# Strassen's seven block products for two in three tiles of the gate and up projections

## The chip, the core and the metric
The kernel runs on one NeuronCore of a Trainium2 chip. The metric is the device time of one execution in microseconds (us). Engines: TensorE (PE; its weight loads are shown apart, as PEld), VectorE (DVE), ScalarE (ACT), GpSimd (POOL), and SyncE (SP), whose queue issues most DMA transfers.

## The reference
One decoder block for 512 tokens of width 1024 in float32: sparse attention and an RWKV-7 branch side by side, merged by gates, then a SwiGLU feed-forward part with 2816 hidden columns. The change is in that last part:

```
hn = _rms_norm(h, ffn_norm[l])
gate, up = _split(hn @ w_gate_up[l], (FFN_HIDDEN, FFN_HIDDEN))
h = h + (jax.nn.silu(gate) * up) @ w_down[l]
```

## The kernel before
Every large product is made of three matmuls: each operand is split into a high part (a copy rounded to the type fp32r, by ScalarE) and a low part (the rest, a subtraction), and high x high, high x low and low x high are summed in PSUM. Weights come as one stream of chunks of 128x1024 (512 KB). `chunk` issues the DMA from SP's queue into one of two raw buffers, has ScalarE make the high part `w_hi`, and has VectorE (every third chunk) or GpSimd make the low part `w_lo`; three buffers each.

The stage around the change begins when the normed hidden state `hn` is there, transposed: 8 blocks of 128 channels by 512 tokens, in high and low parts `hnh` and `hnl`. The 2816 hidden columns are 22 tiles of 128. For a tile, `dense_t` runs 24 matmuls (8 blocks of channels, three each) of 512 columns for gate and 24 for up: weights are held, `hn` is streamed. ScalarE then takes silu of the gate bank (`gsig`), VectorE multiplies it by the up bank (L1108), ScalarE makes the high part `uh`, GpSimd the low part `ul` (L1112). The first three products (tile 0's gate and up, tile 1's gate) are run in halves of 256 columns, as `hn` becomes ready. The down product then holds parts of `uh` and `ul` and streams the weights, in two passes of 512 output columns, with four banks each; at its end VectorE adds the residual and SP writes the output.

PSUM has eight banks: three with tag "d", three "c", two "i". In the gate and up stage only "d" is used.

The order on TensorE is the order of the code (the streams of the attention and the recurrence are done by then). The order on the other engines is set by a scheduler, ahead of time, in one queue per engine; an engine takes its queue in turn. SBUF buffers of one tag are reused in a ring, and the next use waits for the last reader.

Of the kernel before, what the change touches and what calls it, by code (L numbers as in the profile page):

```python
# [10 lines left out]
F32 = mybir.dt.float32  # L11
# [22 lines left out]
UA = ("score", "relu", "widx_t", "tab", "ytile", "sg", "ag", "wa2", "seg", "am", "u32", "ht")  # L34
# [93 lines left out]
def hybrid_block(ctx: ExitStack, tc: tile.TileContext, x, first, rows, consts, lora, rel_bias, stream, out):  # L128
# [10 lines left out]
    def bank(tag, dt=F32, name=None):  # L139
        n = {"d": 3, "i": 2, "c": 3}[tag]  # L140
        return pp.tile([128, 512], dt, name=name or "ps_" + tag, tag=tag, bufs=n)
# [90 lines left out]
    def chunk(k, n):  # L232
# [7 lines left out]
        eng = nc.vector if i >= POOL_ONLY and i % 3 == 0 else nc.gpsimd  # L240
# [7 lines left out]
    def w_tile(n):  # L248

        r = []  # L250
        for _ in range(n // 128):
            r += chunk(1024 // n, n)
        return r
# [734 lines left out]
    def products(wt, w2):  # L988
# [104 lines left out]
        fp = ctx.enter_context(tc.tile_pool(name="ffn", bufs=1))  # L1093
        up = []
        for j in range(NF):
            if j == 0:
                outs = [(bank("d"), w_tile(128)) for _ in range(3)]
                yield from dense_halves(outs, hn, "hn")
                (ps, _), (pu, _), (ps_1, _) = outs
            else:  # L1100
                ps = ps_1 if j == 1 else bank("d")
                if j > 1:
                    yield from dense_t(ps, w_tile(128), slice(0, 128), hn)
                pu = bank("d")
                yield from dense_t(pu, w_tile(128), slice(0, 128), hn)
            g = unit("gsig")
            nc.scalar.activation(g, ps, AF.Silu)
            nc.vector.tensor_mul(g, pu, g)  # L1108
            uh = fp.tile([128, S], F32R, name="uh", tag="uh", bufs=NF)
            ul = fp.tile([128, S], F32R, name="ul", tag="ul", bufs=NF)  # L1110
            nc.scalar.activation(uh, g, AF.Copy)  # L1111
            nc.gpsimd.tensor_sub(ul, g, uh)  # L1112
            up.append((uh, ul))

        for g in range(2):
            cs = slice(g * 512, g * 512 + 512)
            pss = [bank(tag) for tag in (("c", "c", "c", "i") if g == 0 else ("d", "d", "d", "i"))]
            for k0 in range(0, NF, 2):
                wt = chunk(2, 512)
                last = k0 == NF - 2  # L1120
                for t, k in [(t, k) for t in range(NT) for k in range(2)] if last else [(t, k) for k in range(2)
                                                                                   for t in range(NT)]:
                    j, ts = k0 + k, slice(t * 128, t * 128 + 128)
                    uh, ul = up[j][0][:, ts], up[j][1][:, ts]
# [3 lines left out]
                    if j == NF - 1:  # L1128
                        nc.vector.tensor_add(ht[t][g], pss[t], ht[t][g])
                        nc.sync.dma_start(out[t * 128:(t + 1) * 128, cs], ht[t][g])  # L1130

# [92 lines left out]
```

## Time and profile before

| | |
|---|---|
| Time, median of 3 runs | 917.99 us (917.96 to 919.47) |
| The profiled execution's own time | 918.64 us |
| Its span, first to last instruction | 916.9 us |
| Busy: PE, DVE, ACT, POOL | 901.0, 407.5, 345.3, 392.7 us |
| Gate and up products after the halves | 570.08 to 793.15 us |
| Down product to the end | 793.15 to 916.9 us |
| TensorE's granted clock, mean | 0.999 of full (2.4 GHz) |

A matmul's record is longer than the time from its start to the next one's, since matmuls overlap. So a product's time is read from starts, not from the sum of records. An engine's idle time costs something only where TensorE waits for it.

### The profile page before, as it was taken

How to read it: one execution, taken by the hardware profiler on the slowest of the kernel's cores; microseconds unless marked ns; L12 is line 12 of the kernel's file. 1: busy time of each engine (PE TensorE's matmuls, PEld its weight loads, DVE VectorE, ACT ScalarE, POOL GpSimd, SP SyncE). 2: the span in 40 equal slices, each digit the busy share in tenths (PEclk: the TensorE clock that was granted, in tenths of full speed). 3: DMA queues.
4: the chain of work that ended last, by engine and by line, in shares of the span. 5: the costliest groups of instructions: out<-in, count | busy, mean ns of one | idle time of the engine just before them, and what ended most of it. 6: DMA issues, size and time to landing. Idle time of an engine off the chain costs nothing.

```text
span 916.9 us, 13642 instructions
## 1 busy us (share of the span) xinstructions
PE 901.0 (98%) x5550; PEld 760.6 (83%) x5550; DVE 407.5 (44%) x782; ACT 345.3 (38%) x548; POOL 392.7 (43%) x265
## 2 busy tenths in 40 slices
PE   6999999999999999999999999999999999999998
PEld 5988898888787788888888999888888888888886
DVE  5389996785877456756417242111111111110101
ACT  5564575554734333333243243223322232211210
POOL 6477762322572444353338323444344443423321
PEclk9999999999999999999999999999999999999999
DMA  6321332111122111012323222323323222232421
GB/s 239 91 87 46 114 120 71 46 47 38 67 71 60 62 42 48 1 48 81 127 92 94 91 69 82 110 90 110 92 92 107 90 102 93 92 105 88 152 92 46
DMA packets 24173, 77.77 MB, mean 85 GB/s; under 512 B 2869, under 2 KB 4366, under 8 KB 24112
## 3 DMA queue, kind: packets, MB, share of 16 engines
q1 hardware_dynamic: 20688, 72.49, 24.8%
q10 hardware_dynamic: 3424, 4.43, 1.8%
q8 instruction: 43, 0.70, 0.3%
q14 instruction: 18, 0.15, 0.1%
HBM read 74.53 MB, written 2.38 MB: 84 GB/s over the span
## 4 chain that ended last, share of the span: by engine, by line
PE 80%; DVE 3%; POOL 2%; issue 1%; ACT 1%; POOLq 0%; ACTq 0%; DVEq 0%
PE ps_d L162 60%; PE ps_c L162 10%; PE ps_i L162 8%; PE ps_c L169 2%; DVE kr L716 1%; DVE sg L681 1%; POOL w_lo L243 1%; POOL bb L710 0%; PE ps_d L169 0%; POOL ag L719 0%; DVE lg L577 0%; POOL ss L328 0%; DVE xs L330 0%; ACT xs L326 0%; DVE sg L633 0%
## 5 line engine op out<-in xcount | busy, mean ns | idle before, releaser
L243 POOL TENSOR_TENSOR w_lo<-w_raw,w_hi 128x1024 fp32r<-128x1024 f32 (+1 forms) x94 | 223.4, 2377 | 309.9 <-ACT w_hi L239 302.8
L239 ACT ACTIVATE w_hi<-w_raw 128x1024 fp32r<-128x1024 f32 x129 | 136.7, 1060 | 349.3 <-PE ps_d L162 223.0
L162 PE MATMUL ps_d<-hnl,w_hi 128*128 128x512 f32 (+1 forms) x376 | 141.3, 376 | 0.4 <-DVE hnl L338 0.4
L162 PE MATMUL ps_d<-xnl,w_hi 128*128 128x512 f32 (+2 forms) x360 | 141.4, 393 | 0.0
L162 PE MATMUL ps_d<-hnh,w_hi 128*128 128x512 f32 (+1 forms) x376 | 141.2, 376 | 0.0
L162 PE MATMUL ps_d<-hnh,w_lo 128*128 128x512 f32 (+1 forms) x376 | 141.2, 376 | 0.0
L162 PE MATMUL ps_d<-xnh,w_lo 128*128 128x512 f32 (+2 forms) x360 | 140.5, 390 | 0.5 <-POOL w_lo L243 0.5
L162 PE MATMUL ps_d<-xnh,w_hi 128*128 128x512 f32 (+2 forms) x360 | 140.7, 391 | 0.0
L243 DVE TENSOR_TENSOR w_lo<-w_raw,w_hi 128x1024 fp32r<-128x1024 f32 x37 | 48.2, 1302 | 131.1 <-ACT w_hi L239 130.0
L1108 DVE TENSOR_TENSOR gsig<-ps_d,gsig 128x512 f32<-128x512 f32 x22 | 15.2, 692 | 155.0 <-PE ps_d L162 154.3
L162 PEld LDWEIGHTS ps_d<-hnl,w_hi 128*128 128x128 f32 x376 | 70.8, 188 | 13.2 <-DVE hnl L338 0.6
L162 PEld LDWEIGHTS ps_d<-hnh,w_hi 128*128 128x128 f32 x376 | 70.8, 188 | 12.9
L162 PEld LDWEIGHTS ps_d<-hnh,w_lo 128*128 128x128 f32 x376 | 70.7, 188 | 12.8
L162 PEld LDWEIGHTS ps_d<-xnh,w_lo 128*128 128x128 f32 x360 | 68.2, 189 | 12.3 <-issue 1.2
L162 PEld LDWEIGHTS ps_d<-xnl,w_hi 128*128 128x128 f32 x360 | 68.2, 189 | 11.8 <-issue 2.1
L162 PEld LDWEIGHTS ps_d<-xnh,w_hi 128*128 128x128 f32 x360 | 68.3, 190 | 10.7 <-issue 1.2
L1112 POOL TENSOR_TENSOR ul<-gsig,uh 128x512 fp32r<-128x512 f32 x22 | 31.6, 1437 | 24.0 <-ACT uh L1111 20.4
L811 POOL COPY rr<-eye 128x512 f16<-128x512 f16 x20 | 12.6, 635 | 58.2 <-PE ps_i L162 57.3
L162 PE MATMUL ps_d<-w_hi,mh 128*128 128x256 f32 x120 | 34.0, 284 | 0.0
L162 PE MATMUL ps_d<-w_hi,ml 128*128 128x256 f32 x120 | 34.0, 283 | 0.0
L162 PE MATMUL ps_d<-w_lo,mh 128*128 128x256 f32 x120 | 34.0, 283 | 0.0
L584 ACT ACTIVATE lg<-lg,mx,qrs 128x128 f32<-128x128 f32 (+3 forms) x32 | 20.9, 652 | 24.9 <-DVE mx L583 24.9
(294 smaller groups left out, 1712.5 us busy)
## 6 DMA issues: line engine op xcount, KB each, us to landing
w_raw<-in_stream_dram SPq DMA_DIRECT2D x129, 512.0 KB, 3.5
xa<-in_x_dram SPq DMA_DIRECT2D x4, 512.0 KB, 5.9
ht<-in_x_dram ACTq DMA_DIRECT2D x8, 256.0 KB, 3.7
out_dram<-ht SPq DMA_DIRECT2D x8, 256.0 KB, 2.4
toep<-bias_table ACTq DMA_DIRECT2D x8, 128.0 KB, 3.6
gain<-in_rows_dram ACTq DMA_DIRECT2D x2, 256.0 KB, 3.8
con<-in_consts_dram SPq DMA_DIRECT2D x1, 321.0 KB, 6.8
bias_table<-tab ACTq DMA_DIRECT2D x1, 276.0 KB
```

The costliest lines, as they stand in the source:

```text
L162: nc.tensor.matmul(o, w, r, **kw)
L169: nc.tensor.transpose(o, src, idn)
L239: nc.scalar.activation(hi, raw, AF.Copy)
L243: eng.tensor_sub(lo[:, o:o + n_], raw[:, o:o + n_], hi[:, o:o + n_])
L584: nc.scalar.activation(lg, lg, AF.Exp, scale=scale, bias=mx[:, 2:3], accum_out=den[:, h:h + 1])
L681: nc.vector.tensor_tensor_scan(cum, seg, cum, 0.0, op0=OP.mult, op1=OP.add)
L716: nc.vector.tensor_mul(KR[:, :, 0::3], v4(zrp), d3)
L811: nc.gpsimd.tensor_copy(two(R, 1), eye16.rearrange("q (g w s) -> q g w s", w=2, s=s)[:, None, :, 1] .to_broadcast([128, H, 64 // s, s]))
L1108: nc.vector.tensor_mul(g, pu, g)
L1112: nc.gpsimd.tensor_sub(ul, g, uh)
```

## The change
With the gate columns a11, a12 (first and second half of the channels) and the up columns a21, a22 of a tile, and the four blocks b of `hn` (half the channels by half the tokens), gate and up are a 2x2 block product. Strassen's form (Winograd's variant) makes it from seven block products instead of eight, with sums of blocks on both sides.

- `seven_sides`, once: VectorE rebuilds `hn` in float32 (`hnf`, L1227), makes four differences t1 to t4 of its blocks (`tf`, L1236), which ScalarE and VectorE split into high and low parts (`th`, `tl`, L1238 and L1239).
- Tiles 0, 1 and every tile j with j % 3 == 2 stay as they were ("plain"), but their low parts of weights are all on VectorE from tile 2 on. The other 13 tiles (3, 4, 6, 7, ... 18, 19 and 21) are Strassen tiles. For each, the gate chunk comes into `w_raw`, the up chunk into a ring of its own (`wu_raw`); VectorE makes s1 to s4 (L1149 to L1152); seven weight blocks of 128x512 are split, high part on ScalarE (L1155), low part on VectorE (L1156).
- Each of the seven products (`product`) is 12 matmuls with 256 columns. They use four banks: three banks get a second product after the first was read. The sums of products (L1176 to L1192) are on VectorE, two reads on ScalarE are silu and one a copy, and VectorE multiplies gate by up (L1195, L1196).
- All eight PSUM banks are used in turn (`next_bank`).
- The result `up` is kept in float32. The down product splits it again where it is used, in both passes: high part on ScalarE (L1206), low part on VectorE (L1207), in a ring of three buffers, which is that of `wu_raw`.

On TensorE, the place where one product follows another; `hnh` and `hnl` are parts of `hn`, the brackets name whose semaphores are waited for (Activation is ScalarE, Pool is GpSimd, DMAHW a DMA queue). Before, at the switch from a tile's gate to its up product:
```order
L162 MATMUL ps_d<-hnh,w_hi 128x512
L162 MATMUL ps_d<-hnl,w_hi 128x512
L162 MATMUL ps_d<-hnh,w_lo 128x512
L162 MATMUL ps_d<-hnh,w_hi 128x512 [waits Activation_49]
L162 MATMUL ps_d<-hnl,w_hi 128x512
L162 MATMUL ps_d<-hnh,w_lo 128x512 [waits Pool_49]
```
and now, at the end of a Strassen tile's first product and the start of its second, and where its sixth begins:
```order
L162 MATMUL ps_i<-hnl,w_hi 128x256
L162 MATMUL ps_i<-hnh,w_lo 128x256
L162 MATMUL ps_d<-th,w_hi 128x256 [waits Activation_49]
L162 MATMUL ps_d<-tl,w_hi 128x256
L162 MATMUL ps_d<-th,w_lo 128x256 [waits DVE_49]
...
L162 MATMUL ps_i<-hnh,s4h 128x256 [waits DVE_49]
L162 MATMUL ps_i<-hnl,s4h 128x256
L162 MATMUL ps_i<-hnh,s4l 128x256
```
A product has 12 matmuls of half the width in place of 24, so waits for other engines come more often: ten stand in such a tile.

On VectorE, two or three tiles of the gate and up stage before:
```order
L243 TENSOR_TENSOR w_lo<-w_raw,w_hi 128x1024 [waits DMAHW0_49,DVE_49,Activation_49]
L1108 TENSOR_TENSOR gsig<-ps_d,gsig 128x512 [waits PE_49,Activation_49]
L243 TENSOR_TENSOR w_lo<-w_raw,w_hi 128x1024 [waits DVE_49,DMAHW3_49,PE_49,Activation_49]
L1108 TENSOR_TENSOR gsig<-ps_d,gsig 128x512 [waits PE_49,Activation_49] x2
L243 TENSOR_TENSOR w_lo<-w_raw,w_hi 128x1024 [waits DMAHW6_49,DVE_49,Activation_49]
```
and now, from the first tile of a pair (its third and fourth product, `post`) into the second (`L1176` is its second product, `s` and `w_lo` are its weight blocks):
```order
L1182 TENSOR_TENSOR post<-ps_d,post 128x256 [waits DVE_49,PE_49]
L1149 TENSOR_TENSOR s<-wu_raw 128x512 [waits DMAHW6_49]
...
L1188 TENSOR_TENSOR upt<-ps_c,post 128x256 [waits PE_49]
L1156 TENSOR_TENSOR w_lo<-s,w_hi 128x512 [waits Activation_49]
L1152 TENSOR_TENSOR s<-w_raw,s 128x512 [waits DVE_49]
...
L1195 TENSOR_TENSOR u<-gsig,upt 128x256 [waits DVE_49]
L1156 TENSOR_TENSOR s4l<-s,s4h 128x512 [waits Activation_49]
L1176 TENSOR_TENSOR post<-ps_d,post 128x256 [waits PE_49,Activation_49]
L243 TENSOR_TENSOR w_lo<-w_raw,w_hi 128x1024 [waits DMAHW5_49,Activation_49]
L1179 TENSOR_TENSOR post<-ps_i,post 128x256 [waits DVE_49,PE_49]
L1182 TENSOR_TENSOR post<-ps_c,post 128x256 [waits DVE_49,PE_49]
L243 TENSOR_TENSOR w_lo<-w_raw,w_hi 128x1024 [waits DMAHW7_49,Activation_49]
```
The second tile's weight blocks are made between the reads of the first tile's products, and the first low part of the plain tile that follows stands ahead of L1179 and L1182, after whose reads TensorE may write the two banks again.

In the last pair (tiles 18 and 19), the same place on VectorE:
```order
L1176 TENSOR_TENSOR post<-ps_i,post 128x256 [waits PE_49,Activation_49]
L243 TENSOR_TENSOR w_lo<-w_raw,w_hi 128x1024 [waits DMAHW3_49,Activation_49]
L1207 TENSOR_TENSOR us<-u,us 128x512 [waits Activation_49]
L1179 TENSOR_TENSOR post<-ps_c,post 128x256 [waits DVE_49,PE_49]
L243 TENSOR_TENSOR w_lo<-w_raw,w_hi 128x1024 [waits DMAHW4_49,PE_49,Activation_49]
L1182 TENSOR_TENSOR post<-ps_d,post 128x256 [waits DVE_49]
```
Here a low part for the down product (L1207) and the second chunk of the plain tile have moved ahead of the two reads.

The core of the diff (line numbers L11xx and L12xx of the text above are those of the new kernel; L1107 to L1112 are those of the old one, where L1112 of the new one is the multiplication in `plain`):

```diff
-    def chunk(k, n):
+    def chunk(k, n, eng=None):
...
-        eng = nc.vector if i >= POOL_ONLY and i % 3 == 0 else nc.gpsimd
+        eng = eng or (nc.vector if i >= POOL_ONLY and i % 3 == 0 else nc.gpsimd)
...
+        four_k = lambda name, tag, n: fp.tile([128, 4, 256], F32R if tag == "tx" else F32, name=name, tag=tag, bufs=n)
+        tags = ["d", "c", "i", "d", "c", "d", "c", "i"]
         up = []
-        for j in range(NF):
-            if j == 0:
-                outs = [(bank("d"), w_tile(128)) for _ in range(3)]
-                yield from dense_halves(outs, hn, "hn")
-                (ps, _), (pu, _), (ps_1, _) = outs
-            else:
-                ps = ps_1 if j == 1 else bank("d")
-                if j > 1:
-                    yield from dense_t(ps, w_tile(128), slice(0, 128), hn)
-                pu = bank("d")
-                yield from dense_t(pu, w_tile(128), slice(0, 128), hn)
+        def up_rows(j):
+            if j % 2 == 0:
+                up.append(fp.tile([128, 2, S], F32, name="u", tag="u", bufs=NF // 2))
+            return up[j // 2][:, j % 2]
+        turn = [0]
+        def next_bank():
+            turn[0] += 1
+            return bank(tags[(turn[0] - 1) % 8])
+        def plain(j, ps, pu):
             g = unit("gsig")
             nc.scalar.activation(g, ps, AF.Silu)
-            nc.vector.tensor_mul(g, pu, g)
-            uh = fp.tile([128, S], F32R, name="uh", tag="uh", bufs=NF)
-            ul = fp.tile([128, S], F32R, name="ul", tag="ul", bufs=NF)
-            nc.scalar.activation(uh, g, AF.Copy)
-            nc.gpsimd.tensor_sub(ul, g, uh)
-            up.append((uh, ul))
+            nc.vector.tensor_mul(up_rows(j), pu, g)
+        outs = [(bank("d"), w_tile(128)) for _ in range(3)]
+        yield from dense_halves(outs, hn, "hn")
+        quads = seven_sides(fp, four_k, hn_)
+        plain(0, outs[0][0], outs[1][0])
+        pu = next_bank()
+        yield from dense_t(pu, w_tile(128), slice(0, 128), hn)
+        plain(1, outs[2][0], pu)
+        b11, b21, b22, t1, t2, t3, t4 = quads
+        def product(ps, hi, lo, b, first):
+            for k in range(4):
+                ks = slice(k * 128, k * 128 + 128)
+                xh, xl = b[k]
+                mm(ps, hi[:, ks], xh, start=first and k == 0, stop=False, skip_group_check=True)
+                mm(ps, hi[:, ks], xl, start=False, stop=False, skip_group_check=True)
+                mm(ps, lo[:, ks], xh, start=False, stop=k == 3, skip_group_check=True)
+        for j in range(2, NF):
+            if j % 3 == 2:
+                ps, pu = next_bank(), next_bank()
+                yield from dense_t(ps, w_tile(128, nc.vector), slice(0, 128), hn)
+                yield from dense_t(pu, w_tile(128, nc.vector), slice(0, 128), hn)
+                plain(j, ps, pu)
+                continue
+            wg = wp.tile([128, 1024], F32, name="w_raw", tag="w_raw", bufs=WBUFS[0])
+            wu = fp.tile([128, 1024], F32, name="wu_raw", tag="fx", bufs=3)
+            for w in (wg, wu):
+                nc.sync.dma_start(w, stream[at[0]])
+                at[0] += 1
+            a11, a12, a21, a22 = wg[:, 0:512], wg[:, 512:1024], wu[:, 0:512], wu[:, 512:1024]
+            s1, s2, s3, s4 = [unit("s") for _ in range(4)]
+            nc.vector.tensor_add(s1, a21, a22)
+            nc.vector.tensor_sub(s2, s1, a11)
+            nc.vector.tensor_sub(s3, a11, a21)
+            nc.vector.tensor_sub(s4, a12, s2)
+            def split(h, l, w):
+                nc.scalar.activation(h, w, AF.Copy)
+                nc.vector.tensor_sub(l, w, h)
+                return h, l
+            def two(wa, wb):
+                h = wp.tile([128, 1024], F32R, name="w_hi", tag="w_hi", bufs=WBUFS[1])
+                l = wp.tile([128, 1024], F32R, name="w_lo", tag="w_lo", bufs=WBUFS[2])
+                return split(h[:, 0:512], l[:, 0:512], wa), split(h[:, 512:1024], l[:, 512:1024], wb)
+            w11, ws2 = two(a11, s2)
+            ws1, ws3 = two(s1, s3)
+            w12, w22 = two(a12, a22)
+            ws4 = split(fp.tile([128, 512], F32R, name="s4h", tag="s4h", bufs=2),
+                        fp.tile([128, 512], F32R, name="s4l", tag="s4l", bufs=2), s4)
+            pa, pb, pc_, pd = [next_bank()[:, 0:256] for _ in range(4)]
+            post, upt, g = unit("post"), unit("upt"), unit("gsig")
+            u2, u3, c21, u2b = post[:, 0:256], post[:, 256:512], upt[:, 0:256], upt[:, 256:512]
+            product(pa, *w11, b11, True)
+            nc.scalar.activation(u2, pa, AF.Copy)
+            yield 0.0
+            product(pb, *ws2, t2, True)
+            nc.vector.tensor_add(u2, pb, u2)
+            yield 0.0
+            product(pd, *ws1, t1, True)
+            nc.vector.tensor_add(u3, pd, u2)
+            yield 0.0
+            product(pc_, *ws3, t3, True)
+            nc.vector.tensor_add(u3, pc_, u3)
+            yield 0.0
+            product(pa, *w12, b21, False)
+            nc.scalar.activation(g[:, 0:256], pa, AF.Silu)
+            yield 0.0
+            product(pd, *ws4, b22, False)
+            nc.vector.tensor_add(u2b, pd, u2)
+            nc.scalar.activation(g[:, 256:512], u2b, AF.Silu)
+            yield 0.0
+            product(pc_, *w22, t4, False)
+            nc.vector.tensor_add(c21, pc_, u2)
+            yield 0.0
+            u = up_rows(j)
+            nc.vector.tensor_mul(u[:, 0:256], g[:, 0:256], c21)
+            nc.vector.tensor_mul(u[:, 256:512], g[:, 256:512], u3)
         for g in range(2):
             cs = slice(g * 512, g * 512 + 512)
             pss = [bank(tag) for tag in (("c", "c", "c", "i") if g == 0 else ("d", "d", "d", "i"))]
             for k0 in range(0, NF, 2):
                 wt = chunk(2, 512)
+                uu = []
+                for k in range(2):
+                    s = fp.tile([128, 2, S], F32R, name="us", tag="fx", bufs=3)
+                    nc.scalar.activation(s[:, 0], up[k0 // 2][:, k], AF.Copy)
+                    nc.vector.tensor_sub(s[:, 1], up[k0 // 2][:, k], s[:, 0])
+                    uu.append(s)
                 last = k0 == NF - 2
                 for t, k in [(t, k) for t in range(NT) for k in range(2)] if last else [(t, k) for k in range(2)
                                                                                    for t in range(NT)]:
                     j, ts = k0 + k, slice(t * 128, t * 128 + 128)
-                    uh, ul = up[j][0][:, ts], up[j][1][:, ts]
+                    uh, ul = uu[k][:, 0, ts], uu[k][:, 1, ts]
                     mm(pss[t], uh, wt[k][0], start=(j == 0), stop=False)
                     mm(pss[t], uh, wt[k][1], start=False, stop=False)
                     mm(pss[t], ul, wt[k][0], start=False, stop=(j == NF - 1))
                     if j == NF - 1:
                         nc.vector.tensor_add(ht[t][g], pss[t], ht[t][g])
                         nc.sync.dma_start(out[t * 128:(t + 1) * 128, cs], ht[t][g])
+    def seven_sides(fp, four_k, a):
+        f = []
+        for q in range(4):
+            f.append(fp.tile([128, 2, S], F32, name="hnf", tag="u", bufs=NF // 2))
+            s = slice(2 * (q % 2), 2 * (q % 2) + 2)
+            nc.vector.tensor_add(f[q], a[0][q // 2][:, s], a[1][q // 2][:, s])
+        def block(k, t):
+            return [f[2 * k + e][:, :, 256 * t:256 * t + 256] for e in range(2)]
+        def minus(x, y):
+            d = four_k("tf", "u", NF // 2)
+            r = [d[:, 2 * e:2 * e + 2] for e in range(2)]
+            for e in range(2):
+                nc.vector.tensor_sub(r[e], x[e], y[e])
+            h, l = four_k("th", "tx", 8), four_k("tl", "tx", 8)
+            nc.scalar.activation(h, d, AF.Copy)
+            nc.vector.tensor_sub(l, d, h)
+            return r, [(h[:, k], l[:, k]) for k in range(4)]
+        d1, t1 = minus(block(0, 1), block(0, 0))
+        d2, t2 = minus(block(1, 1), d1)
+        _, t3 = minus(block(1, 1), block(0, 1))
+        _, t4 = minus(block(1, 0), d2)
+        as_is = lambda k, t: [(a[0][k][:, i, 256 * t:256 * t + 256], a[1][k][:, i, 256 * t:256 * t + 256])
+                              for i in range(4)]
+        return as_is(0, 0), as_is(1, 0), as_is(1, 1), t1, t2, t3, t4
```

## Rows read from the trace of the kernel before

**Rows 1.** The page: span, totals of the engines, and the chain that ended last.
```profile
span 916.9 us, 13642 instructions
PE 901.0 (98%) x5550; PEld 760.6 (83%) x5550; DVE 407.5 (44%) x782; ACT 345.3 (38%) x548; POOL 392.7 (43%) x265
...
PE ps_d L162 60%; PE ps_c L162 10%; PE ps_i L162 8%; PE ps_c L169 2%; DVE kr L716 1%; DVE sg L681 1%; POOL w_lo L243 1%; POOL bb L710 0%; PE ps_d L169 0%; POOL ag L719 0%; DVE lg L577 0%; POOL ss L328 0%; DVE xs L330 0%; ACT xs L326 0%; DVE sg L633 0%
```

**Rows 2.** Windows: us, then busy and (count) of PE, PEld, DVE, ACT, POOL; clock, DMA.
```profile
570.08:793.15 223.07, 223.07 (x987) 184.69 (x985) 30.99 (x34) 64.98 (x82) 95.23 (x49) 1.00 0.32 100
793.15:917.00 123.85, 119.84 (x529) 98.91 (x527) 13.58 (x15) 21.80 (x21) 34.77 (x15) 0.99 0.29 94
```

**Rows 3.** Timeline, 512-column matmuls (start, us, engine, line, names): first, last of a product, next stage.
```profile
570.08 0.40 PE L162 MATMUL ps_d<-hnh,w_hi 128*128 128x512 f32 x1
...
575.32 0.39 PE L162 MATMUL ps_d<-hnh,w_lo 128*128 128x512 f32 x1
575.82 0.69 DVE L1108 TENSOR_TENSOR gsig<-ps_d,gsig 128x512 f32<-128x512 f32 x1 [7.66 <-PE ps_d L162]
...
793.15 0.39 PE L162 MATMUL ps_c<-w_hi,uh 128*128 128x512 f32 x1
```

**Rows 4.** Timeline, 256-column matmuls, first and last of 44.
```profile
564.80 0.28 PE L162 MATMUL ps_d<-hnl,w_hi 128*128 128x256 f32 x1
...
569.96 0.28 PE L162 MATMUL ps_d<-hnh,w_lo 128*128 128x256 f32 x1
```

**Rows 5.** Window in the output projection, 256-column matmuls alone.
```profile
506.00:540.00 34.00, 34.00 (x285) 1.00 0.30 92
```

**Rows 6.** The matmul's line in 508 to 538 us (ns min/median/max, first and last start).
```profile
L162 PEld LDWEIGHTS ps_d<-w_lo,mh x84: 192/192/192, 507.9 to 537.8; 128*128 128x128 f32 x84
...
L162 PEldq EVENT_SEMAPHORE  x2: 51/51/51, 521.2 to 532.7; - x2
```

**Rows 7.** Timeline, a matmul that came late, and the next.
```profile
549.40 0.38 PE L162 MATMUL ps_d<-hnl,w_hi 128*128 128x256 f32 x1 [0.41 <-DVE hnl L338]
549.62 0.28 PE L162 MATMUL ps_d<-hnh,w_lo 128*128 128x256 f32 x1
```

**Rows 8.** VectorE's groups by form (busy us, mean ns); the first in gate and up alone.
```profile
L243 DVE TENSOR_TENSOR w_lo<-w_raw,w_hi 128x1024 fp32r<-128x1024 f32 x14 | 17.2, 1225 | 40.0 <-ACT w_hi L239 39.5
...
L1085 DVE TENSOR_TENSOR ht<-ps_d,ht 128x256 f32<-128x256 f32 x15 | 5.8, 419 | 18.9 <-PE ps_d L162 18.9
...
L717 DVE TENSOR_TENSOR kb<-ag,inv 128x512 f32<-128x512 f32 x4 | 2.8, 689 | 0.1
```

**Rows 9.** Timeline, VectorE instructions close behind each other.
```profile
134.44 0.68 DVE L446 MAX8 max<-score 128x8 f32<-128x512 f32 x1
135.04 0.19 DVE L583 TENSOR_SCALAR mx<-mx,qrs 128x1 f32<-128x1 f32 x1
...
137.99 0.34 DVE L573 SCALAR_TENSOR_TENSOR lg<-toep,qrs,ps_c 128x128 f32<-128x128 f32 x1
138.37 0.29 DVE L574 TENSOR_REDUCE mx<-lg 128x1 f32<-128x128 f32 x1
...
512.04 0.76 DVE L1085 TENSOR_TENSOR ht<-ps_d,ht 128x256 f32<-128x256 f32 x2 [2.12 <-PE ps_d L162]
```

**Rows 10.** ScalarE's group of 512-column copies.
```profile
L1111 ACT ACTIVATE uh<-gsig 128x512 fp32r<-128x512 f32 x22 | 13.9, 632 | 0.0
```

**Rows 11.** Timeline at the stage's start, VectorE's and ScalarE's.
```profile
556.51 1.43 DVE L338 TENSOR_TENSOR hnl<-ps_c,hnh 128x512 fp32r<-128x512 f32 x2 [0.71 <-ACT hnh L337]
...
564.45 1.06 ACT L239 ACTIVATE w_hi<-w_raw 128x1024 fp32r<-128x1024 f32 x1 [7.24 <-PE ps_d L162]
...
566.82 0.60 ACT L1107 ACTIVATE gsig<-ps_d 128x512 f32<-128x512 f32 x1
```

**Rows 12.** DMA issues by line (KB each, median us to landing), the page's and the stage's.
```profile
xa<-in_x_dram SPq DMA_DIRECT2D x4, 512.0 KB, 5.9
...
w_raw<-in_stream_dram SPq DMA_DIRECT2D x44, 512.0 KB, 3.5
```

More of the change, by code (lines that the diff above doesn't have):

```diff
@@ L33 @@
 UNITS, WBUFS = {"ua": 10, "uc": 8}, (2, 3, 3)
-UA = ("score", "relu", "widx_t", "tab", "ytile", "sg", "ag", "wa2", "seg", "am", "u32", "ht")
+UA = ("score", "relu", "widx_t", "tab", "ytile", "sg", "ag", "wa2", "seg", "am", "u32", "ht", "upt")
 SMALL = {"ss": 4, "max8": 3, "mx": 4}
@@ L246, in chunk, with w_tile @@
         return [(h3[:, j], l3[:, j]) for j in range(k)]
-    def w_tile(n):
+    def w_tile(n, eng=None):
         r = []
         for _ in range(n // 128):
-            r += chunk(1024 // n, n)
+            r += chunk(1024 // n, n, eng)
         return r
```

## The prediction

> **What bounds the kernel now.** I read the page's totals and chain first, then the stages by windows, then single matmuls and VectorE instructions in time. TensorE is busy 901.0 of a span of 916.9 us, and its matmul line L162 alone makes up 78% of the chain that ended last (60, 10 and 8% by the three kinds of PSUM bank) [rows 1]. The gate and up products run from 570.08 to 793.15 us, and in those 223.07 us TensorE is never idle, while VectorE works 30.99 us and ScalarE 64.98 us [rows 2]. So in that stage only the number and the spacing of the matmuls count. The stage holds 41 products of 24 matmuls, 984 in all: 223.07 / 984 = 0.2267 us from one start to the next, for matmuls of 512 columns. A matmul's record (0.39 us) is longer than its spacing, because matmuls overlap; all sums below go by spacing.
>
> Matmuls of 256 columns have a spacing of their own. From 564.80 to 569.96 us 43 of them follow each other with the same operands as here (weights held, activations streamed): 5.16 / 43 = 0.1200 us [rows 4]. In the output projection 285 fit into 34.00 us, 0.1193 us [rows 5]. Half the columns thus cost 53% of the time, not 50%.
>
> **The change, part by part.** *Matmuls.* Of the 22 column tiles, 13 (two of every three from tile 3 on) get seven products of 12 matmuls with 256 columns, 84, in place of 48 with 512. Per tile: 48 x 0.2267 = 10.88 us before, 84 x 0.1200 = 10.08 after, 0.80 saved; for 13 tiles 10.4 us. The stage becomes 360 x 0.2267 + 1092 x 0.1200 = 212.6 us. With 0.1193 instead it is 11.2 us saved; that is the lower end. An eighth of the columns goes away (84 x 256 against 48 x 512), 12.5% of 10.88 or 1.36 us; the dearer halves take 0.56 of that back.
>
> The new form has 36 more weight loads per tile. A load's record is 0.192 us, longer than the 0.12 us between two matmuls of 256 columns, and yet the spacing stays at 0.1193 to 0.1200 [rows 4 to 6]: the loads lie beside the matmuls. The Trainium skill, "TensorE: Matmul & The Clock Gate", section "The mechanism", says that a weight load overlaps with running matmuls only where its row group differs. All loads here fill the same rows, so by that rule they would lie on the path; the trace disagrees, with 0.12 us between matmuls whose loads alone take 0.19 us, and the rule is left a small chance below.
>
> *VectorE.* A Strassen tile gives it 11 instructions of 128x512 out of SBUF (4 sums of weight blocks, 7 low parts), 5 of 128x256 that read PSUM and 2 of 128x256 in SBUF. Rows of before show 0.689 us for the first kind and 0.419 for the second [rows 8]; with 0.419 for the third too the sum is 11 x 0.689 + 7 x 0.419 = 10.5 us per tile, above TensorE's 10.08. But instructions that follow each other without a dependence start sooner than the one before ends: 0.60 us apart for a 0.68 us one, and two of 128x256 take 0.76 together, so 0.34 apart; dependent ones stand 0.38 apart for a duration of 0.34, 0.04 behind the end [rows 9]. By spacing the tile costs 11 x 0.60 + 7 x 0.34 = 9.0 us. A plain tile costs it 2 x 1.14 + 0.60 = 2.9 (1.225 us [rows 8] less the same 0.08), so a group of three 20.9 us beside 31.0 us of TensorE. On average it fits; what matters is the order within a pair, since VectorE takes its instructions in turn. The Trainium skill, "VectorE: DVE Perf Modes", section "The DRAIN you can't avoid", has the next operation wait until the pipeline is empty. The spacing of 0.60 us under a duration of 0.68 does not agree with that; by that rule the tile costs the 10.5 us, which is the second case below.
>
> The tight place is the second tile of a pair. Time 0 is the start of the first one; products last 1.44 us; VectorE can read a product 0.50 us after the start of its last 512-column matmul, 0.11 after that record's end [rows 3], so with a 0.28 us record 0.27 us after the product's last spacing. VectorE in the order of the listing: L1182 waits for product 4 and starts at 6.03; s1 to s3 at 6.37, 7.10, 7.70; L1188 waits for product 6, 8.91; L1156 9.25; s4 9.85; the low part of s2 10.45, ends 11.14. The second tile's product 2 needs it at its third matmul, 10.08 + 1.44 + 0.24 = 11.76: 0.6 us to spare. On it goes: L1192 11.05, low part 11.39, L1196 11.99, low parts 12.33 and 12.93, L1195 13.53, low part of s4 13.87, L1176 14.47, the plain tile's 1024-wide low part 14.81, L1179 15.95 to 16.37. Product 6 writes again into the bank which L1179 reads and starts at 10.08 + 7.2 = 17.28: 0.9 us to spare. ScalarE copies in 0.63 us (512 columns) and 1.06 (1024) [rows 10, 11], seven copies of 512 and three reads of 256 columns per tile, well under the 10.08; its copy for the plain tile can start when product 2 is through at 13.2 and ends at 14.3, before VectorE wants it. So in five of the six pairs I cost the sums and splits at nothing; they lie beside the matmuls, and the cover is VectorE's overlap.
>
> The last pair (tiles 18 and 19) has two more instructions ahead of those reads, as the listing shows. The first low part for the down product (L1207, 0.60) leaves 0.3 of the 0.9 us. The second L243 stands ahead of L1182. Its raw chunk goes into the buffer that is free when the second tile's low part of a12 is made, at 13.0; a chunk lands 3.5 us later [rows 12], ScalarE 1.06, L243 1.23, L1182 0.42: 19.2 us, and product 7 waits for it at 10.08 + 8.64 = 18.72. Cost 0.5 us. A landing of 5.9 us, the slowest near row for such a chunk [rows 12], would make it 2.9; a quick one, nothing. I take 0.5, since 44 chunks have that median.
>
> *Preparation.* VectorE gets 4 sums of 1024, 8 differences of 512 and 4 low parts of 1024, after the last hnl, which ends at 556.51 + 1.43 = 557.94 [rows 11]. Eleven of them stand ahead of tile 1's low part: 4 x 1.14 + 7 x 0.62 = 8.9, then 1.23, ends 568.1; its first use is the third matmul from 570.08, 570.55. With full durations it ends 568.9. Hidden, with 1.6 us to spare or more. ScalarE makes the same first copy at 564.45, and the silu that frees the bank for 570.08 ran from 566.82 to 567.42 [rows 11]; one copy of 1.06 is put ahead of it, so it ends by 568.5. The other low parts are done near 578, and the first Strassen tile starts at 570.08 + 72 x 0.2267 = 586.4.
>
> *Down product.* Each of 44 row tiles is now split again there: ScalarE 0.63 and VectorE 0.69 per 12 matmuls (2.72 us), beside 1.06 and a third of 1.23 per two tiles. Both stay under half busy; the ring of three gives a buffer back two row tiles, 5.4 us, ahead of its need, and the refill takes about 1.5. Cost 0. GpSimd loses its low parts in the gate and up stage, which were on no path. SP moves the same 44 chunks in that stage; the up chunk of a Strassen tile gets a buffer of its own and is issued ahead, and the 100 GB/s of the stage [rows 2] stay.
>
> **Sum.** -10.4 + 0.5 = -9.9 us. Against the profiled execution's own 918.64 us (its span 916.9 and 1.7 around it) that is 908.7. The runs shown have a median 0.65 lower, 917.99, so I predict 908.1. Less than 0.2% (1.8 us) could not be told from no change.
>
> **The rivals.** *VectorE does not overlap in such a mixed queue.* With full durations the same walk gives L1179's end at 17.47, 0.2 us late; and if each of the some 18 instructions with their waits takes 0.05 more, 1.1 late. Six pairs lose 1.2 to 6.6 us, the last one about 1 more: 909 to 915, in the middle 912.5. For it: nearly every one of these instructions waits for another engine, and the rows of overlap are from a stretch with fewer waits. Against: that stretch was dense too [rows 9].
>
> *Nothing gained.* The plain tile's gate chunk stands in VectorE's queue ahead of both reads that the second tile waits for. If it comes late, each pair stalls; 1.65 us per pair gives 918. It may take 13 us from its issue to landing before it costs anything, and 14.7 for this; 3.5 is the row. Unlikely.
>
> *Slower: each wait on TensorE's own queue costs.* When a matmul really was late (549.40), its successor came 0.22 us later, not 0.12: 0.10 lost beside the wait itself [rows 7]. The listing has ten waits in a Strassen tile. If each costs 0.10 even when met in time, the tile takes 11.08 us against 10.88, 13 tiles lose 2.6, with the last pair 3.1: 921. It decides from 0.08 us per wait (0.80 / 10). Against it: the stretch of rows 5 has waits of 0.05 us on the queue that loads the weights [rows 6], and the gate and up stage has two or three per product; neither left a mark in the spacing.
>
> *Slower by far: weight loads on the path.* 36 more loads of 0.19 less 0.80 us, for 13 tiles: +78 us, 996. The spacing in rows 4 speaks against it.
>
> **How the numbers follow.** Forecast 0.70; VectorE without overlap 0.18; nothing gained 0.05; waits that cost 0.06; loads on the path 0.01. Faster is the first two, 0.88; same 0.05; slower 0.07. The range starts at 906.0 (0.1193 us spacing and no stall: 906.2) and reaches to 914.0, which takes in most of the second case.
>
> **What would show it.** In the changed kernel's trace: 1092 matmuls of 128x256 at 0.120 us in the gate and up stage; the stage 212.6 us plus small gaps; the one clear gap at products 6 and 7 of tile 19; the down product again 120 us from its first to its last matmul, without gaps. Gaps in TensorE at the second product or at products 6 and 7 of every second Strassen tile, released by VectorE, would show the second case; a longer spacing only behind waits, the slower one. I am wrong if VectorE's starts in the pairs stand further apart than 0.60 and 0.34 us, or if TensorE's spacing in the seven products isn't 0.120.

## The result, and the profile after

The changed kernel takes 909.16 us (median of 4 runs, 908.4 to 910.07); the kernel before, run beside it, took 918.47 (4 runs). The ratio is 0.9896, with a 95% interval of 0.9884 to 0.9907. The prediction was 908.1 (906 to 914), faster.

From the page of the kernel after, the line of engine totals (busy us, share of the span, instructions) and the chain by lines; they answer to [rows 1]:

```profile
PE 891.5 (98%) x6018; PEld 775.3 (85%) x6018; DVE 572.6 (63%) x1064; ACT 394.0 (43%) x665; POOL 296.6 (33%) x216
...
PE ps_d L162 48%; PE ps_c L162 19%; PE ps_i L162 14%; PE ps_c L169 2%; DVE score L447 2%; DVE max L446 2%; POOL w_lo L243 1%; DVE kr L716 1%; DVE sg L681 1%; DVE qs L470 1%; PE ps_i L169 0%; DVE score L427 0%; DMA grow<-in_rows_dram 0%; POOL bb L710 0%; POOL ag L719 0%
```

TensorE has 468 more matmuls and is 9.5 us less busy; VectorE has 165 us more. L162, now spread over three kinds of bank, still makes up 81% of the chain (78% before): the bound is the same engine. Two windows of after, cut where the first 512-column matmul of the gate and up stage and the first of the down product start (columns as in [rows 2]):

```profile
570.84:784.17 213.33, 213.03 (x1454) 198.65 (x1453) 151.30 (x262) 89.22 (x159) 2.41 (x1) 1.00 0.30 96
784.17:907.90 123.73, 119.87 (x530) 98.95 (x528) 48.28 (x58) 45.03 (x61) 33.54 (x14) 1.00 0.32 98
```

The stage went from 223.07 to 213.33 us, the down product (to the end) from 123.85 to 123.73. In the stage TensorE lacks 0.30 us of being always busy. VectorE went from 30.99 to 151.30 us, GpSimd from 95.23 to 2.41. The stage began 0.76 us later than in the profile of before; the kernels of the experiments began it between 569.53 and 570.92, and in after VectorE's last two `hnl`, ahead of the first new instruction, already start at 557.28 where before had 556.51. So this is put down to the single execution.

The spacing: TensorE's timeline of after, from a product in tile 21 to the first matmul of the down product (start, us, names):

```profile
779.85 0.28 PE L162 MATMUL ps_i<-hnh,w_hi 128*128 128x256 f32 x1
...
784.17 0.40 PE L162 MATMUL ps_c<-w_hi,us 128*128 128x512 f32 x1
```

36 steps in 4.32 us, 0.1200 us each, across three products and their bank changes.

VectorE's timeline of after in the pair of tiles 6 and 7, behind the matmul with which tile 6 starts; it answers to the walk of the prediction:

```profile
618.25 0.28 PE L162 MATMUL ps_d<-hnh,w_hi 128*128 128x256 f32 x1
...
624.20 0.42 DVE L1182 TENSOR_TENSOR post<-ps_i,post 128x256 f32<-128x256 f32 x1 [1.02 <-PE ps_i L162]
...
627.08 0.42 DVE L1188 TENSOR_TENSOR upt<-ps_d,post 128x256 f32<-128x256 f32 x1 [0.53 <-PE ps_d L162]
627.42 0.68 DVE L1156 TENSOR_TENSOR w_lo<-s,w_hi 128x512 fp32r<-128x512 f32 x1
628.02 0.69 DVE L1152 TENSOR_TENSOR s<-w_raw,s 128x512 f32<-128x512 f32 x1
...
632.64 0.41 DVE L1176 TENSOR_TENSOR post<-ps_i,post 128x256 f32<-128x256 f32 x1
632.97 1.21 DVE L243 TENSOR_TENSOR w_lo<-w_raw,w_hi 128x1024 fp32r<-128x1024 f32 x1
634.10 0.41 DVE L1179 TENSOR_TENSOR post<-ps_c,post 128x256 f32<-128x256 f32 x1
```

From 618.25 the VectorE lines are at 5.95, 8.83, 9.17, 9.77, 14.39, 14.72 and 15.85; the walk had 6.03, 8.91, 9.25, 9.85, 14.47, 14.81 and 15.95. Each of these starts is 0.08 to 0.10 us ahead of the walk, and from start to start the two agree within 0.02. The other five pairs have the same times within 0.02 up to the L243 of their 14.72.

The last pair (tiles 18 and 19), ScalarE, VectorE and TensorE of after around the one gap:

```profile
758.95 1.06 ACT L239 ACTIVATE w_hi<-w_raw 128x1024 fp32r<-128x1024 f32 x1 [1.85 <-DMA w_raw<-in_stream_dram]
...
758.34 0.68 DVE L1207 TENSOR_TENSOR us<-u,us 128x512 fp32r<-128x512 f32 x1
758.94 0.41 DVE L1179 TENSOR_TENSOR post<-ps_c,post 128x256 f32<-128x256 f32 x1
760.04 1.23 DVE L243 TENSOR_TENSOR w_lo<-w_raw,w_hi 128x1024 fp32r<-128x1024 f32 x1 [0.68 <-ACT w_hi L239]
761.18 0.42 DVE L1182 TENSOR_TENSOR post<-ps_d,post 128x256 f32<-128x256 f32 x1
...
761.08 0.28 PE L162 MATMUL ps_c<-hnh,s4l 128*128 128x256 f32 x1
761.65 0.39 PE L162 MATMUL ps_d<-th,w_hi 128*128 128x256 f32 x1 [0.29 <-DVE post L1182]
761.88 0.28 PE L162 MATMUL ps_d<-tl,w_hi 128*128 128x256 f32 x1
```

ScalarE's copy waits for the chunk to land until 758.95, the second L243 waits for the copy, L1182 stands behind it, and product 7 of tile 19 starts 0.57 us after its predecessor in place of 0.12: 0.45 us, then 0.11 more at the restart (0.23 to the next start), 0.56 in all. It is the only matmul of the stage that waited for another engine.

### The profile page after: what moved, and what is told of

Its sections match the earlier page's. It is cut to its first block, busy times and chain, and to the rows that moved or that the text cites. A ratio compares the mean times of both kernels' runs of the same rounds, so it can differ in the third digit from the quotient of the medians.

```text
span 907.9 us, 14949 instructions
## 1 busy us (share of the span) xinstructions
PE 891.5 (98%) x6018; PEld 775.3 (85%) x6018; DVE 572.6 (63%) x1064; ACT 394.0 (43%) x665; POOL 296.6 (33%) x216
## 4 chain that ended last, share of the span: by engine, by line
PE 84%; DVE 9%; POOL 2%; issue 2%; ACT 2%; DMA 1%; ACTq 0%; POOLq 0%; DVEq 0%
PE ps_d L162 48%; PE ps_c L162 19%; PE ps_i L162 14%; PE ps_c L169 2%; DVE score L447 2%; DVE max L446 2%; POOL w_lo L243 1%; DVE kr L716 1%; DVE sg L681 1%; DVE qs L470 1%; PE ps_i L169 0%; DVE score L427 0%; DMA grow<-in_rows_dram 0%; POOL bb L710 0%; POOL ag L719 0%
## 5 line engine op out<-in xcount | busy, mean ns | idle before, releaser
L243 POOL TENSOR_TENSOR w_lo<-w_raw,w_hi 128x1024 fp32r<-128x1024 f32 (+1 forms) x67 | 158.5, 2368 | 421.3 <-ACT w_hi L239 414.1
L239 ACT ACTIVATE w_hi<-w_raw 128x1024 fp32r<-128x1024 f32 x103 | 108.7, 1056 | 129.5 <-PE ps_d L162 93.9
L162 PE MATMUL ps_d<-xnl,w_hi 128*128 128x512 f32 (+2 forms) x360 | 141.4, 393 | 0.0
L162 PE MATMUL ps_d<-xnh,w_lo 128*128 128x512 f32 (+2 forms) x360 | 140.6, 390 | 0.4 <-POOL w_lo L243 0.4
L162 PE MATMUL ps_d<-xnh,w_hi 128*128 128x512 f32 (+2 forms) x360 | 140.7, 391 | 0.0
L162 PEld LDWEIGHTS ps_d<-xnh,w_lo 128*128 128x128 f32 x360 | 68.2, 189 | 12.2 <-issue 1.2
L162 PEld LDWEIGHTS ps_d<-xnl,w_hi 128*128 128x128 f32 x360 | 68.2, 190 | 11.8 <-issue 2.1
L162 PEld LDWEIGHTS ps_d<-xnh,w_hi 128*128 128x128 f32 x360 | 68.3, 190 | 10.7 <-issue 1.2
L1207 DVE TENSOR_TENSOR us<-u,us 128x512 fp32r<-128x512 f32 x44 | 36.7, 835 | 64.2 <-ACT us L1206 64.2
L243 DVE TENSOR_TENSOR w_lo<-w_raw,w_hi 128x1024 fp32r<-128x1024 f32 x38 | 49.2, 1296 | 18.9 <-ACT w_hi L239 18.3
L1206 ACT ACTIVATE us<-u 128x512 fp32r<-128x512 f32 x44 | 27.8, 632 | 67.4 <-PE ps_i L162 67.2
L162 PE MATMUL ps_d<-hnl,w_hi 128*128 128x256 f32 (+1 forms) x144 | 46.0, 319 | 0.4 <-DVE hnl L338 0.4
L162 PE MATMUL ps_d<-hnh,w_hi 128*128 128x256 f32 (+1 forms) x144 | 45.9, 319 | 0.0
L162 PE MATMUL ps_d<-hnh,w_lo 128*128 128x256 f32 (+1 forms) x144 | 45.9, 319 | 0.0
L162 PE MATMUL ps_c<-w_hi,us 128*128 128x512 f32 x132 | 44.1, 389 | 0.0
L162 PE MATMUL ps_d<-w_hi,us 128*128 128x512 f32 x132 | 44.1, 389 | 0.0
L1156 DVE TENSOR_TENSOR w_lo<-s,w_hi 128x512 fp32r<-128x512 f32 x39 | 26.1, 685 | 22.2 <-ACT w_hi L1155 22.2
L162 PE MATMUL ps_d<-w_hi,mh 128*128 128x256 f32 x120 | 34.0, 284 | 0.0
L162 PE MATMUL ps_d<-w_hi,ml 128*128 128x256 f32 x120 | 34.0, 283 | 0.0
L162 PE MATMUL ps_d<-w_lo,mh 128*128 128x256 f32 x120 | 34.0, 283 | 0.0
L162 PE MATMUL ps_i<-w_hi,us 128*128 128x512 f32 x88 | 33.9, 389 | 0.0
```

The costliest lines, as they stand in the source:

```text
L162: nc.tensor.matmul(o, w, r, **kw)
L239: nc.scalar.activation(hi, raw, AF.Copy)
L243: eng.tensor_sub(lo[:, o:o + n_], raw[:, o:o + n_], hi[:, o:o + n_])
L1156: nc.vector.tensor_sub(l, w, h)
L1206: nc.scalar.activation(s[:, 0], up[k0 // 2][:, k], AF.Copy)
L1207: nc.vector.tensor_sub(s[:, 1], up[k0 // 2][:, k], s[:, 0])
```

## The experiments

The theory: in this stage only the number and the spacing of matmuls count, and VectorE's work is hidden because its starts come 0.60 and 0.34 us apart. The rivals that the result alone doesn't exclude: the gain comes from somewhere else (waits, the freed GpSimd, the down product), or VectorE is near to binding, or the product order doesn't matter. "Over after" below is against 909.16 (the kernel before took 918.47 beside it, and 918.67 or 918.60 beside the experiments).

**All tiles from 3 on by seven products.**
```diff
-            if j % 3 == 2:
+            if j == 2:
```


> Tiles 5, 8, ... 20 are Strassen tiles too (19 instead of 13). Theory (only TensorE's spacing counts, VectorE's starts 0.60 and 0.34 us apart hide the rest): in a row of Strassen tiles L1182 still waits for product 4, so each tile begins its walk anew and none stalls; 6 x 0.80 = 4.8 us less than the changed kernel, 904 to 905 us. Rival (the plain tile in between is what lets VectorE catch up): without it VectorE, 9.0 to 10.5 us of work per 10.08 us tile, falls behind and TensorE waits in every tile; 909 us or more.


Measured 904.02 us (903.38 to 904.82), 0.9837 of before [0.9816, 0.9858]. Its window over the stage:
```profile
570.53:778.72 208.19, 208.11 (x1671) 205.09 (x1669) 186.42 (x352) 100.91 (x201) 2.40 (x1) 1.00 0.30 98
```
Against 213.33 the stage lost 5.14 us for six more tiles. Of this 0.56 is the gap of after's last pair, which is gone, and 0.34 is spent in a new one (below), so the tiles gave 4.9, 0.82 each. VectorE's records fill 186 of 208 us, and one matmul waited for it, product 6 of tile 21. GpSimd, VectorE and TensorE there:
```profile
772.40 2.40 POOL L243 TENSOR_TENSOR w_lo<-w_raw,w_hi 128x1024 fp32r<-128x1024 f32 x1 [217.60 <-ACT w_hi L239]
...
772.88 2.48 DVE L1207 TENSOR_TENSOR us<-u,us 128x512 fp32r<-128x512 f32 x1 [0.34 <-ACT us L1206]
775.27 0.41 DVE L1179 TENSOR_TENSOR post<-ps_c,post 128x256 f32<-128x256 f32 x1
...
775.38 0.28 PE L162 MATMUL ps_d<-hnh,w_lo 128*128 128x256 f32 x1
775.74 0.39 PE L162 MATMUL ps_c<-hnh,s4h 128*128 128x256 f32 x1
```
Beside GpSimd's first low part for the down product, VectorE's L1207 takes 2.48 us in place of 0.68 (758.34 in after), and it stands ahead of the bank's read: 0.36 us between the two matmuls in place of 0.12, and 0.10 at the restart. This kernel beats both others.

**The same work before, in halves.** In the kernel before, the 26 products of the 13 tiles are made as two halves of 256 columns.
```diff
+                split = j > 1 and j % 3 != 2
...
+                    for t in (0, 256) if split else (0,):
+                        yield from dense_t(ps[:, t:t + (256 if split else S)], wt, ...
...
```


> The kernel before, with the gate and up products of the 13 tiles run as two halves of 256 columns each (no block products, nothing else changed). Theory (a 256-column matmul costs 0.1200 us, not half of 0.2267): 96 x 0.1200 - 48 x 0.2267 = 0.64 us more per tile, 13 tiles 8.3 us: 926 to 927 us. Rival (columns alone count, and the missing part of the 17.7 us that an eighth fewer columns would give is lost in waits): no change, 918.5 us.


Measured 926.59 (926.33 to 927.01), ratio 1.0083 [1.0058, 1.0107]: +7.9 against the 918.67 beside it. Its window over the stage:
```profile
569.53:801.03 231.50, 231.50 (x1610) 217.32 (x1609) 31.00 (x34) 64.40 (x82) 95.72 (x49) 1.00 0.32 96
```
The stage is 8.43 us longer than before's 223.07, without a gap. 48 matmuls per tile become pairs of halves, at 2 x 0.1200 - 0.2267 = 0.0133 more each: 0.64 per tile, 8.3 for 13. This is the price of narrow matmuls alone; an eighth fewer of them pays 18.7 us (13 x 12 x 0.1200) on top of it.

**Only the down product's splitting.** All tiles plain, `up` kept in float32 and split again in the down product.
```diff
-            if j % 3 == 2:
+            if True:
```
(and without `seven_sides`)


> The changed kernel with all 22 tiles plain: no block products, but up kept in float32 and split again in both passes of the down product, low parts of weights from tile 2 on VectorE, all eight banks in turn. Theory (the second split is hidden, ScalarE and VectorE stay under half busy there): 918.5 us as before, within 1 us. Rival (the ring of three is too short, or the start of the passes waits): 919.5 to 922, and the changed kernel would have gained that much more without it.


Measured 918.76 (918.01 to 919.38), ratio 0.9998 [0.9989, 1.0008]; its stage takes 223.07 us, as before's. GpSimd's low parts gave nothing back when they went, and the new splits cost nothing.

**Two uses of a bank next to each other.** The order of products is a, b, d, d, c, c, a instead of a, b, d, c, a, d, c.
```diff
-            product(pc_, *ws3, t3, True)
-            nc.vector.tensor_add(u3, pc_, u3)
...
-            product(pa, *w12, b21, False)
-            nc.scalar.activation(g[:, 0:256], pa, AF.Silu)
...
             product(pd, *ws4, b22, False)
...
+            product(pc_, *ws3, t3, True)
+            nc.vector.tensor_add(u3, pc_, u3)
...
             product(pc_, *w22, t4, False)
...
+            product(pa, *w12, b21, False)
+            nc.scalar.activation(g[:, 0:256], pa, AF.Silu)
```


> The changed kernel with another order of the seven products: pa, pb, pd, pd again, pc, pc again, pa again, so that two banks get their second product right behind their first. Theory (the order hides the read of a bank before it is written again): twice per tile TensorE waits for the first product to drain (0.27 us), VectorE's read (0.42) and the restart (up to 0.10), 1.4 to 1.7 us per tile, 13 tiles 18 to 22 us: 927 to 931 us, slower than the kernel before. Rival (the order is of no account, VectorE's supply of low parts decides): 909 us.


Measured 935.61 (935.49 to 936.01), ratio 1.0181 [1.016, 1.0201]: 26.5 us over after, 2.04 per tile where 1.4 to 1.7 was expected. Its timeline, TensorE at two second uses in tiles 6 and 7, and VectorE ahead of the later one:
```profile
625.94 0.28 PE L162 MATMUL ps_d<-th,w_lo 128*128 128x256 f32 x1
626.83 0.35 PE L162 MATMUL ps_d<-hnh,s4h 128*128 128x256 f32 x1 [0.61 <-DVE post L1179]
627.02 0.28 PE L162 MATMUL ps_d<-hnl,s4h 128*128 128x256 f32 x1
...
637.91 0.28 PE L162 MATMUL ps_c<-th,w_lo 128*128 128x256 f32 x1
639.47 0.36 PE L162 MATMUL ps_c<-hnh,s4h 128*128 128x256 f32 x1 [1.28 <-DVE post L1179]
...
637.76 1.22 DVE L243 TENSOR_TENSOR w_lo<-w_raw,w_hi 128x1024 fp32r<-128x1024 f32 x1 [0.48 <-ACT w_hi L239]
638.90 0.42 DVE L1179 TENSOR_TENSOR post<-ps_c,post 128x256 f32<-128x256 f32 x1
```
With VectorE free, a bank's next product starts 0.89 us after the last matmul in place of 0.12, and the matmul behind it 0.19 later: 0.84 lost. With the 1.2 us L243 ahead of the read it is 1.56, 1.51 lost with the restart; behind a sum of weight blocks, in the first tile of each pair, it is 1.11. The expectation had counted the first and not VectorE's queue ahead of the read. The order of the changed kernel, two or three products between a bank's uses, is worth 26 us.

**Each low part twice on VectorE.**
```diff
-                nc.vector.tensor_sub(l, w, h)
+                for _ in range(2):
+                    nc.vector.tensor_sub(l, w, h)
```


> Each of the seven low parts of a Strassen tile is computed twice on VectorE (7 more instructions of 128x512 per tile, the result is unchanged); TensorE's order is unchanged. It tells apart whether VectorE's work is counted by the spacing of its starts or by durations, and whether the order within a pair or the average binds. Theory (by spacing, 0.60 us each, in the walk of the prediction): the second tile's L1179 comes 7 x 0.60 = 4.2 us later than 16.4, less about 0.6 of waiting that is filled, so 2.7 us past the 17.28 at which product 6 wants its bank: 6 pairs lose 16 us and some restarts, 925 to 929 us, although the average of a group of three (20.9 + 8.4 = 29.3 of 31.0 us) would still fit. Rival A (only the average counts): 909 to 911. Rival B (full durations, 0.69 us each, no overlap in the mixed queue): 5.0 us per pair, 936 to 941.


Measured 931.71 (930.89 to 934.41), ratio 1.0147 [1.013, 1.0163]: 22.6 over after. It lies between the first case and rival B, and the place was wrong. TensorE at product 2 of tile 7, and VectorE ahead of it:
```profile
633.82 0.28 PE L162 MATMUL ps_i<-tl,w_hi 128*128 128x256 f32 x1
636.98 0.38 PE L162 MATMUL ps_i<-th,w_lo 128*128 128x256 f32 x1 [2.88 <-DVE w_lo L1157]
...
634.70 0.69 DVE L1157 TENSOR_TENSOR w_lo<-w_raw,w_hi 128x512 fp32r<-128x512 f32 x1
635.30 0.69 DVE L1157 TENSOR_TENSOR w_lo<-wu_raw,w_hi 128x512 fp32r<-128x512 f32 x1
...
636.23 0.69 DVE L1157 TENSOR_TENSOR w_lo<-s,w_hi 128x512 fp32r<-128x512 f32 x1
```
The starts are 0.60 apart here too, so the mixed queue overlaps and rival B's mechanism is out; rival A, which counted only the average, is out as well. But the scheduler put the second copies behind other low parts, and the one that product 2 needs ends at 636.92, so TensorE waits there already, before the bank of L1180 matters. Five such gaps of 3.16 us and one of 3.61, less the 0.12 of a spacing, are 18.7 us; five restarts add 0.5. After two of the six the granted clock fell; windows of that kernel over the gap, and behind it (columns as before), first and sixth gap:
```profile
598.20:601.30 3.10, 0.26 (x3) 0.06 (x1) 3.10 (x7) 0.81 (x3) 0.00 (x0) 0.99 0.00 0
601.30:604.50 3.20, 3.16 (x15) 3.16 (x16) 3.20 (x6) 0.79 (x1) 0.00 (x0) 0.50 0.01 1
...
770.60:774.20 3.60, 0.27 (x4) 0.07 (x2) 3.60 (x8) 1.25 (x4) 0.00 (x0) 1.00 0.00 0
774.20:777.50 3.30, 3.30 (x20) 3.30 (x21) 3.30 (x6) 1.48 (x2) 0.00 (x0) 0.67 0.27 71
```
The second fall came 1.2 us after the gap's end. At 0.50, the lower of the two levels (1.2 GHz), a step takes 0.213 us; 14 steps from 601.34 to 604.50 (a restart of 0.38 among them) take 3.16 us and 15 from 775.35 to 778.55 take 3.20: together 2.9 us lost. The sum 18.7 + 0.5 + 2.9, less the 0.56 of the gap that after has, is 21.5; the stage (570.20 to 805.13) is 21.6 us longer than after's 213.33. Without the clock the time would have been some 928.8, inside the 925 to 929 of the first case, but by waits at another product: that would have been luck.

**Low parts on GpSimd.**
```diff
-                nc.vector.tensor_sub(l, w, h)
+                nc.gpsimd.tensor_sub(l, w, h)
```


> The seven low parts of a Strassen tile go to GpSimd instead of VectorE; everything else as in the changed kernel. GpSimd took 1.445 us for a 128x512 low part in the kernel before, so a tile costs it 7 x 1.445 = 10.1 us, as long as the tile's matmuls (10.08), and VectorE keeps 4 sums, 5 reads and 2 products, 4.8 us. Theory: a walk with 1.445 us each has the second tile's low parts done at about 9.9, 11.4, 12.8, 14.3, 15.7 and 17.2 us for needs at 11.8, 13.2, 14.6, 16.1, 17.5 and 19.0, so there is over a microsecond of reserve and the plain tile lets GpSimd catch up: within 1.5 us of the changed kernel, 908 to 911. Rival: two engines that work at once on SBUF lengthen each other (a VectorE low part takes 0.835 us in the down product beside GpSimd, against 0.69); at over 1.6 us per low part GpSimd falls behind in every pair and TensorE waits for w_lo: 913 to 925.


Measured 911.12 (910.93 to 911.33), ratio 0.9918 [0.9903, 0.9932]: 2.0 over after, just outside the theory's 1.5 and below the rival. GpSimd, VectorE and TensorE in the pair of tiles 6 and 7 (tile 6 starts at 618.17 here):
```profile
632.38 2.34 POOL L1156 TENSOR_TENSOR w_lo<-wu_raw,w_hi 128x512 fp32r<-128x512 f32 x1
634.69 1.28 POOL L1156 TENSOR_TENSOR s4l<-s,s4h 128x512 fp32r<-128x512 f32 x1
...
629.75 1.51 DVE L1195 TENSOR_TENSOR u<-gsig,upt 128x256 f32<-128x256 f32 x1
632.35 1.23 DVE L243 TENSOR_TENSOR w_lo<-w_raw,w_hi 128x1024 fp32r<-128x1024 f32 x1 [0.53 <-ACT w_hi L239]
...
635.56 0.28 PE L162 MATMUL ps_c<-hnl,s4h 128*128 128x256 f32 x1
636.02 0.38 PE L162 MATMUL ps_c<-hnh,s4l 128*128 128x256 f32 x1 [0.18 <-POOL s4l L1156]
```
Where both engines work out of SBUF, the one that starts later takes longer: GpSimd's low part of a22, just behind the start of L243, takes 2.34 us (1.31 in the first tile of the pair), and L1195 beside a low part 1.51 (0.42 in after). On average a low part takes 1.41 us, not the rival's 1.6. In each pair the low part of s4, last in GpSimd's queue and behind the long one, ends at 17.8 after the pair's start where the expectation had 17.2, late for product 6: 0.46 us between starts in place of 0.12, and 0.10 at the restart, 0.44 times six, 2.6, less the 0.56 of after's own gap: the 2 us. The expectation had also set s4's need too late: the needs in GpSimd's order are 16.1, 19.0 and 17.5, so it had 0.3 us in reserve and not 1.8.

**Tile 2 too.**
```diff
-            if j % 3 == 2:
+            if j < 0:
```


> Tile 2 too is made by seven products (20 Strassen tiles, none plain but 0 and 1). It tests the preparation's cover: in the changed kernel the seven sides and low parts had until 587 us; here tile 2 starts at about 576.5. Theory: VectorE is through with the sides by about 575 and the low part of s2 is ready near 577.7 for a need at 578.0, later low parts are within 1 us of theirs: one more 0.8 us is gained less a short wait, 903 to 904.5 us against 904.0 with 19 tiles. Rival: the preparation isn't through, TensorE waits 2 us or more at tile 2, 905 to 909.


Measured 906.01 (904.9 to 907.09), ratio 0.986 [0.9844, 0.9877]: 2 us above the kernel with 19 tiles. The rival's time and wait hold, though by the order of the low parts and not by late sides. TensorE at tile 2's second product, and VectorE:
```profile
577.70 0.28 PE L162 MATMUL ps_c<-hnh,w_lo 128*128 128x256 f32 x1
578.15 0.39 PE L162 MATMUL ps_i<-th,w_hi 128*128 128x256 f32 x1 [0.17 <-ACT w_hi L1155]
...
580.48 0.38 PE L162 MATMUL ps_i<-th,w_lo 128*128 128x256 f32 x1 [1.82 <-DVE w_lo L1156]
...
574.39 1.22 DVE L1239 TENSOR_TENSOR tl<-tf,th 128x1024 fp32r<-128x1024 f32 x1
...
579.73 1.29 DVE L1156 TENSOR_TENSOR w_lo<-s,w_hi 128x512 fp32r<-128x512 f32 x2
```
The sides end at 575.6, near the 575 expected, but the low part of s2 stands behind those of a12 and a22 and is made at 579.73; I had taken the first `w_lo<-s` of the queue, at 577.33, for it. TensorE loses 0.33, 1.99 and two restarts of 0.10, 2.5 us, where 0.8 was to be had. The reserve of the preparation, wide in the changed kernel, is used up one plain tile earlier.

## Why the prediction was right

- *Matmuls, -10.4.* Stage forecast: 212.6 + 0.5 = 213.1; measured 213.33. The 0.1200 of [rows 4] held to the last digit. The stage without its gap gives 0.79 per tile ((223.07 - 213.33 + 0.56) / 13). The runs show both parts of it: narrowing alone costs 0.65 per tile (8.43 / 13, halves; 0.61 by the medians), seven products on all tiles give 0.82 per further tile (forecast 0.80).
- *Weight loads beside the matmuls.* 0.1200 us between matmuls that each have a load of 0.19 us ahead; the rival at 996 is out. The sentence of the Trainium skill, "TensorE: Matmul & The Clock Gate", section "The mechanism", that a load overlaps with running matmuls only where its row group differs does not agree with any run here. The same section also has a load pulled ahead when it targets the background weight buffer, which the prediction left out; whether that is what happens here no run shows.
- *VectorE hidden by its overlap.* From start to start the walk came out within 0.02 us up to L1179. One term of it was mis-sized: VectorE reads a product 0.19 us after its last spacing (L1182 at 5.95 for a product that ends at 5.76), not 0.27, so the starts lie 0.08 to 0.10 earlier. L1179's record ended at 16.26, against a need at 17.27: 1.0 us to spare and not 0.9. The rival by full durations (912.5) is out: starts 0.60 apart in after and, under double load, still 0.60. The Trainium skill, "VectorE: DVE Perf Modes", section "The DRAIN you can't avoid", also says that a next operation which is not held starts earlier. The 0.60 us under a duration of 0.68 agree with that sentence, and not with the wait that the prediction took from the section. How close it was is shown by the doubled low parts: seven more instructions per tile cost 22.6 us (2.9 of them by the clock) although the average fits.
- *Last pair, +0.5.* The gap is at product 7 of tile 19 behind the second L243, as said: 0.45, or 0.56 with the restart. The walk had L1182 start at 18.8 after the pair's start; with product 7 due at 761.20 that start is 742.48, and 761.18 is 18.70. The chunk was there at 16.47, for 16.5 in the sum. That is one landing of one execution: the mechanism is shown, but that the size came out so well is in part luck, since by the prediction's own rows a slower landing makes it 2.9 and a quick one nothing.
- *Preparation and down product, 0.* No wait of TensorE in either. The down product alone was timed at a ratio of 0.9998. Its L1207 took 846 ns, not 689, with GpSimd at work beside it; the cover was wide enough.
- *Waits on TensorE's queue (921).* The spacing stays 0.1200 across products with their waits met, so a met wait costs nothing; a missed one costs 0.07 to 0.11 at the restart, near the 0.10 of [rows 7].
- What was off is 1.0 us: the profiled execution took 909.72 for a forecast of 908.7. Of that 0.76 is the later start of the stage, which the change doesn't touch, and 0.2 the stage. The sum behind the low end has a slip: 917.99 - 11.2 is 906.8, not 906.2; the range's 906 lies below both.

## What to carry to other kernels

Count a trade of fewer for narrower matmuls by the measured spacing of both widths, and not by columns: here an eighth fewer columns shortened a tile by 0.79 of 10.88 us, 7%. Then walk the helper engine's queue in its own order, by starts and not by durations, up to each need: the average fits long before the order does, and one instruction of 1.2 us ahead of a bank's read raised the loss from 0.84 to 1.51 us. When some of the work is moved to a cheaper form, try it on all of it: the tiles left plain as relief for VectorE were not needed, which was worth another 5 us.

## What the runs showed of the hardware that was not expected

- VectorE and GpSimd, both at work out of SBUF, lengthen each other by far more than expected, in the cases shown the one that starts later: VectorE's L1207 (128x512) took 2.48 us in place of 0.68 beside a GpSimd instruction that still had 1.9 to run, GpSimd's low part 2.34 in place of 1.31 beside an L243 that had 1.2 to run and itself stayed at 1.23. VectorE's reads of PSUM stayed at 0.42 us.
- TensorE's clock fell to half behind one of five idle stretches of 2.88 us, and 1.2 us after the end of one of 3.33 us: 14 or 15 matmuls mostly 0.213 us apart in place of 0.12, 1.4 to 1.5 us lost each time. The longest idle stretch in the stages of the other runs, 1.82 us (tile 2 too), brought no fall.
- A bank that is read by VectorE and written again at once costs TensorE 0.77 us over the spacing, with the reader idle, and 0.07 more at the restart.
